# Key and value caches in layouts made by kernel(), outputs stored from the loaded tiles, tail reordered: one step of a two-layer decoder on one core

## The chip, the cores and the metric

The kernel runs on one core of one Trainium2 chip. The core has TensorE (PE: matmuls, with a weight load PEld for each), VectorE (DVE), ScalarE (ACT), GpSimd (POOL) and SyncE (SP). SP issues nearly all DMAs here, in its program order; the DMAs then run on the core's 16 DMA engines. The metric is device time in microseconds, from start to end of one execution. What kernel() does with numpy on the host, before and after the launch, isn't in it.

## The reference

One inference step for a prompt of 256 tokens (with 16 learned meta tokens ahead of it, 272 positions) and for a group of 8 samples of one token each. Layer 0 is an RWKV-7 mixer, layer 1 is sliding-window attention with grouped queries and sinks. Both layers have width 4096 (model width 2048), and each branch is gated. All data is fp32.

```python
if i == N_A_LAYERS - 1:
    kp, vp = shared_kv(hp, kv_norm, w_kv, pos_p)          # prompt: keys after rotary, values
    ksn, vsn = shared_kv(hs, kv_norm, w_kv, pos_s)        # samples: the new key and value
    k_all = jnp.concatenate([cache_k.astype(ksn.dtype), ksn], axis=1)   # (8, 128 + 1, 8, 64)
    v_all = jnp.concatenate([cache_v.astype(vsn.dtype), vsn], axis=1)
...
q, z = jnp.split(rmsnorm(hp, b_norm[j]) @ b_w_qz[j], 2, axis=-1)
q = rotary(q.reshape(B, L, N_Q_HEADS, HEAD_DIM), pos_p)
att = banded_prompt_attention(q, kp, vp, sinks)
hp = hp + (att * jax.nn.silu(z)) @ b_w_o[j]
...
att = sink_attend(q, k_all, v_all, valid_s, sinks).reshape(DB, S_dec, WIDTH)
hs = hs + (att * jax.nn.silu(z)) @ b_w_o[j]
...
y_prompt = rmsnorm(hp, final_norm)[:, N_META:]
y_sample = rmsnorm(hs, final_norm)
p_cache_k = kp[:, -win:]
p_cache_v = vp[:, -win:]
s_cache_k = k_all[:, -win:]
s_cache_v = v_all[:, -win:]
```

The cache that goes in has 128 positions for each sample, 8 key heads of 64 and as many values. The cache that goes out has the same size: the oldest position is dropped, the new one is put at the end. Queries are 64 heads, 8 to each key head.

## The kernel before

**Products.** Every large product is made with split fp32: a weight tile of 256 x 256 (256 KB, `raw`) is loaded by SP (L192 in `wunits`), ACT rounds it to `whi` (L177), VectorE makes the rest `wlo` (L178), and `mm3` does three matmuls, high by high, high by low, low by high (L199, L200, L201). A tile, called a unit here, is worth 12 matmuls. There are 4 buffers of raw (8 in most of the attention part, with the second pool `rawx`) and 5 each of whi and wlo, so ACT and VectorE work a few units ahead of TensorE, and SP about eight ahead.

**Stages.** `phase_a` is the RWKV mixer, `out_a` its output product. `phase_b` makes the shared keys and values: four products of `kv`, then for each pair of key heads `rotate` on VectorE (`stream_shuffle`, three operations; the result is the tile `rout_k`), and copies to `KT` (keys transposed, 64 rows twice, 280 positions). Keys come out of the product with head dimension on the partitions. For the outputs that want position on the partitions, TensorE transposes them (`ps_kt`, L1446 and L1447, against the identity in `consts`), VectorE copies the result to `ktk` and `ksn` (L1448, L1449), and SP stores those.

**Attention.** `phase_b2` runs the query and gate products (q, z) and, in between, a generator `heads`: for each of 8 groups (key heads) and each half of a group, two planes of scores (`ps_s`), a softmax on VectorE and ACT, the transposes of the probabilities (`ps_pt`) and the values (`ps_at`). TensorE's order here is the order in which the generators are run, written out by hand; `yield 5`, say, is five steps of the product, half a unit each. `end_q` rotates a plane of queries on VectorE as soon as its product is done; the scores of the plane wait for that.

The samples' attention is `attend_cache(g)`, run in five parts by `heads`. The first part loads the cache of group g (`kc` and `vc`, 128 positions on the partitions, L1718 and L1719) and copies 127 positions of sample g from the input cache to the output cache, DRAM to DRAM (L1723). The second spreads the queries (`qz`), transposes kc (`ps_kc`, L1737, four matmuls), copies the result to `kTc` by ACT (L1739) and puts the new key into kTc's last column by VectorE (L1742). The third makes scores (`ps_dc`, L1746) and their softmax (`dm`, `dSB`). The fourth transposes the probabilities (`ps_dp`), the fifth makes the values (`ps_da`). There are two buffers of kc and vc, one of kTc.

**What sets the order elsewhere.** On VectorE, ACT, GpSimd and SP, and on TensorE outside the handwritten stretches, a scheduler with a cost model orders the instructions at build time. Each engine then runs its list strictly in order: what stands behind a waiting instruction waits too.

**The tail.** `out_b` is the last output product, 16 column blocks k, two to a product. For each it adds the residual, squares (`sqb`, ACT), sums the squares of blocks 0 to 14 on GpSimd (`sqacc`, L1804), transposes the block (`ps_h`, L1807) and scales it into `ht` (L1810). Row sums of squares come from matmuls with ones (`ps_stb`, L1813): one set for sqacc at k = 14, one for the last block's squares at k = 15. Then an inverse root by VectorE, a scaling of ht[0] by VectorE (L1823) and of ht[1] by ACT (L1825) in two halves of 1024 columns, and the stores (L1824, L1826, L1828).

Of the kernel before, what the change touches and what calls it, by code (L numbers as in the profile page):

```python
# [10 lines left out]
F32 = mybir.dt.float32  # L11
# [13 lines left out]
NS = 8  # L25
# [78 lines left out]
class Kernel:  # L104
# [1300 lines left out]
    def phase_b(self):  # L1405
# [21 lines left out]
        with self.tc.tile_pool(name="kvm", bufs=2, reuse_waits="tile") as pool:  # L1427
# [3 lines left out]
            dma(cs, I['consts'][:, C_COS:C_COS + 2 * N].rearrange("p (a n) -> p a n", a=2))  # L1431
            ksn, ktk = (pool.tile([r, 512], F32, tag=n, bufs=1, name=n) for r, n in ((NS, "ksn"), (128, "ktk")))
            tt(cosr, cs[:, 0], self.rb, op=MU)
            tt(sinr, cs[:, 1], self.rb, op=MU)
            for c in range(4):
                if c % 2 == 0:
                    pss = self.gemm(I['w_kv'][0], "kv", KT, c * 128, x)
                    self.pump(c == 2)
                ps = pss[c % 2]
                kr = self.rotate(pool, ps, cosr, sinr, N, f"k{c}")  # L1440
                for h in range(2):
                    s = slice(64 * h, 64 * h + 64)
                    for q in range(2):
                        (V.tensor_copy if q else A.copy)(self.KTd[2 * c + h][64 * q:64 * q + 64], kr[s])
                pt = self.bank(self.pe, f"ps_kt{c}")
                nc.tensor.transpose(pt[:, 0:128], kr[:, 144:272], self.ident)  # L1446
                nc.tensor.transpose(pt[:NS, 128:256], kr[:, L:N], self.ident)  # L1447
                V.tensor_copy(ktk[:, c * 128:c * 128 + 128], pt[:, 0:128])  # L1448
                V.tensor_copy(ksn[:, c * 128:c * 128 + 128], pt[:NS, 128:256])  # L1449
            for c in range(4):  # L1450
# [18 lines left out]
            dma(self.Vm[16:32, :, 64:128], self.Vm[:16, :, 0:64])  # L1469
            f = lambda n: O[n].rearrange("b w h d -> b w (h d)")  # L1470
            dma(f('p_cache_k')[0], ktk)
            dma(f('p_cache_v')[0], self.Vd)
            dma(f('s_cache_k')[:, WIN - 1], ksn)
            dma(O['s_cache_v'][:, WIN - 1], self.Vn[0:64:8, :, 0])
            self.bmx = [self.norm_mix(bp, "bm", P_BN, k) for k in range(KT)]
# [236 lines left out]
    def attend_cache(self, g):  # L1712

        nc, bp, I = self.nc, self.bp, self.I
        V, A = nc.vector, nc.scalar
        kc = bp.tile([128, NS, 64], F32, tag="kc", bufs=2, name=f"kc{g}")
        vc = bp.tile([128, NS, 64], F32, tag="vc", bufs=2, name=f"vc{g}")
        nc.sync.dma_start(kc, I['cache_k'][:, :, g].rearrange("b w d -> w b d"))  # L1718
        nc.sync.dma_start(vc, I['cache_v'][:, :, g].rearrange("b w d -> w b d"))  # L1719
        for n in 'kv':  # L1720
            row = lambda a: a[g].rearrange("w h d -> w (h d)")
            self.tc.keep_in_program_order(
                nc.sync.dma_start(row(self.O['s_cache_' + n])[0:WIN - 1], row(I['cache_' + n])[1:WIN]))  # L1723
        yield
# [4 lines left out]
        for o in range(2):  # L1729
            for h in range(2):  # L1730
                c = 8 * o + h
                V.tensor_copy(qz.rearrange("p (s c) -> p s c", c=144)[64 * o:64 * o + 64, :, c:c + 8:2],
                              qs[64 * h:64 * h + 64, o])
        kT = bp.tile([128, NS // 2, 129], F32, tag="kTc", name=f"kTc{g}")
        pk = self.bank(self.py, f"ps_kc{g}")
        for i in range(4):
            nc.tensor.transpose(pk[:, 128 * i:128 * i + 128], kc[:, 2 * i:2 * i + 2].rearrange("p b d -> p (b d)"),  # L1737
                                self.ident)
        A.copy(kT[:, :, 0:128], pk.rearrange("p (b w) -> p b w", b=4))  # L1739
        for o in range(2):  # L1740
            r = slice(64 * o, 64 * o + 64)
            V.tensor_copy(kT[r, :, 128], self.KTd[g][r, L + o:N:2])  # L1742
        yield
        pd = self.bank(self.py, f"ps_dc{g}")[:, :129]
# [34 lines left out]
    def out_b(self):  # L1779
# [11 lines left out]
        for k in range(KT):  # L1791
# [8 lines left out]
            if k == 0:  # L1800
                acc = pool.tile([128, NB], F32, name="sqacc")
                nc.gpsimd.tensor_copy(acc, sq)
            elif k < KT - 1:
                nc.gpsimd.tensor_tensor(acc, acc, sq, op=ALU.add)  # L1804
# [3 lines left out]
            for i, r in enumerate(rows):  # L1808
                s = slice(128 * k, 128 * k + 128)
                V.tensor_tensor(ht[i][:r, s], pt[:r, 128 * i:128 * i + 128], fn[:r, s], op=ALU.mult)  # L1810
            if k >= KT - 2:
                for i, r in enumerate(rows):
                    nc.tensor.matmul(pst[i][:r, 0:2], (acc if k == KT - 2 else sq)[:, 128 * i:128 * i + r], one,  # L1813
                                     start=k == KT - 2, stop=k == KT - 1)
        rs = pool.tile([128, 3], F32, name="rsf")
# [4 lines left out]
        outs = (O['y_prompt'][0, 0:128], O['y_prompt'][0, 128:256], O['y_sample'].rearrange("b o d -> (b o) d"))  # L1820
        for c in range(2):
            s = slice(D // 2 * c, D // 2 * c + D // 2)
            V.tensor_scalar(ht[0][:, s], ht[0][:, s], rs[:, 0:1], None, op0=ALU.mult)  # L1823
# [8 lines left out]
    ('y_prompt', (1, SEQ, D)), ('y_sample', (NS, 1, D)), ('p_state_wkv', (1, 1, 64, 64, 64)),  # L1832
    ('p_state_shift', (1, 1, D)), ('p_cache_k', (1, WIN, NKV, HD)), ('p_cache_v', (1, WIN, NKV, HD)),
    ('s_state_wkv', (1, NS, 64, 64, 64)), ('s_state_shift', (1, NS, D)),
    ('s_cache_k', (NS, WIN, NKV, HD)), ('s_cache_v', (NS, WIN, NKV, HD)),
]
# [7 lines left out]


# [16 lines left out]
```

## Time and profile before

| | |
|---|---|
| median of 3 runs | 2201.3 us (2196.46, 2201.3, 2201.85) |
| the profiled execution's own time | 2204.44 us |
| its span, first to last instruction | 2202.5 us |
| mean granted TensorE clock | 0.987 |
| DMA moved | 455.40 MB, 207 GB/s over the span |

| stage, us of the span | what |
|---|---|
| 0 to 1456 | start, RWKV mixer and its output product |
| 1456.8 to 1515.1 | keys and values |
| 1515.1 to 1997.3 | q and z products, with attention from 1529 to 1901 |
| 1997.3 to 2188.3 | last output product |
| 2188.3 to 2202.5 | tail |

How to read it: the page gives busy time by engine, in sum and by stretch; PEclk is the clock that TensorE was granted, as a share of full speed. Matmuls are pipelined, so one may stand for 0.28 us while the next starts 0.12 us after it. Rows of the timeline are: start, how long, engine, line, operation, tiles out and in, shapes, count, and in brackets the idle time ahead of it with what ended that. Rows of waits are: who waited for what, microseconds in total, times, longest. In lists of instructions, "x32: 271/272/273" is the count and the shortest, median and longest nanoseconds. Rows that start with a stretch (A:B) give busy time of PE, PEld, DVE, ACT and POOL in it, then clock, DMA's share and GB/s.

### The profile page before, as it was taken

The numbers are of one execution on the slowest core, as the hardware profiler recorded it, in microseconds if no ns is written. First come the engines' busy times: TensorE is split into PE (matmuls) and PEld (weight loads), VectorE is DVE, ScalarE is ACT, GpSimd is POOL, SyncE is SP. The second block draws the span as 40 slices with busy tenths as digits, with TensorE's granted clock in tenths as the row PEclk, the third lists the DMA queues.
The fourth block names the chain that finished last, engine by engine and source line by source line (L and its number), as shares of the span: only waits on it lengthen the run. The fifth ranks groups of instructions, "written<-read, shape, count | busy, mean of one in ns | idle before, by whom it ended". The sixth has DMA issues, their size and how long they took to land. (4 is left out here: it accounts for less than half of the span.)

```text
span 2202.5 us, 56367 instructions
## 1 busy us (share of the span) xinstructions
PE 2124.8 (96%) x21596; PEld 2015.7 (92%) x21596; DVE 1710.4 (78%) x4138; ACT 1284.0 (58%) x2961; POOL 76.5 (3%) x102
## 2 busy tenths in 40 slices
PE   6999999999999999989999999999999999999997
PEld 4899889899999899989988999999999999999997
DVE  5875757687678677689877787887888888888885
ACT  3546766577676666667766544565555556555443
POOL 0010000000000000000100000110000000000000
PEclk9999999999999999999999999999999999999999
DMA  7978566668676658766655868777554544577774
GB/s 239 340 260 257 173 229 210 198 174 266 204 220 187 188 187 268 239 208 184 200 175 150 283 177 278 240 212 207 163 159 140 163 150 134 163 212 242 229 226 136
DMA packets 289718, 455.40 MB, mean 207 GB/s; under 512 B 64280, under 2 KB 112984, under 8 KB 289056
## 3 DMA queue, kind: packets, MB, share of 16 engines
q1 hardware_dynamic: 288632, 449.51, 66.0%
q8 instruction: 169, 2.77, 0.5%
q10 hardware_dynamic: 816, 2.29, 0.3%
q14 instruction: 101, 0.83, 0.1%
HBM read 385.08 MB, written 70.73 MB: 207 GB/s over the span
## 5 line engine op out<-in xcount | busy, mean ns | idle before, releaser
L199 PE MATMUL ps_z<-mhlm,whi_z 128*128 128x280 f32 x512 | 160.0, 312 | 0.0
L201 PE MATMUL ps_z<-mhlm,wlo_z 128*128 128x280 f32 x512 | 151.5, 296 | 0.8 <-DVE wlo_z L178 0.8
L199 PE MATMUL ps_q<-bmh,whi_qb 128*128 128x264 f32 x512 | 150.0, 293 | 1.5 <-ACT whi_qb L177 1.5
L200 PE MATMUL ps_z<-mhlm,whi_z 128*128 128x280 f32 x512 | 151.2, 295 | 0.0
L199 PE MATMUL ps_z<-bmh,whi_zb 128*128 128x264 f32 x512 | 147.5, 288 | 0.0
L201 PE MATMUL ps_q<-bmh,wlo_qb 128*128 128x264 f32 x512 | 145.8, 285 | 1.1 <-DVE wlo_qb L178 1.1
L200 PE MATMUL ps_q<-bml,whi_qb 128*128 128x264 f32 x512 | 145.6, 284 | 0.0
L200 PE MATMUL ps_z<-bml,whi_zb 128*128 128x264 f32 x512 | 145.5, 284 | 0.0
L201 PE MATMUL ps_z<-bmh,wlo_zb 128*128 128x264 f32 x512 | 145.4, 284 | 0.0
L199 PE MATMUL ps_ob<-ghi,whi_ob 128*128 128x264 f32 x512 | 145.3, 285 | 0.0
L201 PE MATMUL ps_ob<-ghi,wlo_ob 128*128 128x264 f32 x512 | 144.8, 285 | 0.0
L200 PE MATMUL ps_ob<-glo,whi_ob 128*128 128x264 f32 x512 | 144.5, 283 | 0.0
L177 ACT CAST whi_ob<-raw_ob 128x512 fp32r<-128x512 f32 x128 | 79.2, 621 | 97.1 <-PE ps_ob L200 82.1
L178 DVE TENSOR_TENSOR wlo_r<-raw_r,whi_r 128x512 fp32r<-128x512 f32 x128 | 86.8, 686 | 57.1 <-ACT whi_r L177 51.7
L177 ACT CAST whi_oa<-raw_oa 128x512 fp32r<-128x512 f32 x128 | 78.3, 620 | 87.2 <-DMA raw_oa<-a_w_out 27.1
L178 DVE TENSOR_TENSOR wlo_v<-raw_v,whi_v 128x512 fp32r<-128x512 f32 x128 | 86.7, 685 | 50.8 <-ACT whi_v L177 49.2
L199 PE MATMUL ps_v<-mhlm,whi_v 128*128 128x280 f32 x384 | 121.9, 317 | 0.0
L199 PE MATMUL ps_k<-mhlm,whi_k 128*128 128x280 f32 x384 | 121.2, 316 | 0.0
L178 DVE TENSOR_TENSOR wlo_k<-raw_k,whi_k 128x512 fp32r<-128x512 f32 x112 | 76.5, 690 | 56.8 <-ACT whi_k L177 54.8
L177 ACT CAST whi_zb<-raw_zb 128x512 fp32r<-128x512 f32 x128 | 78.3, 620 | 62.5 <-PE ps_z L200 41.1
L178 DVE TENSOR_TENSOR wlo_z<-raw_z,whi_z 128x512 fp32r<-128x512 f32 x128 | 86.5, 683 | 36.3 <-ACT whi_z L177 36.0
L200 PE MATMUL ps_k<-mhlm,whi_k 128*128 128x280 f32 x384 | 113.8, 296 | 0.0
(479 smaller groups left out, 7726.0 us busy)
## 6 DMA issues: line engine op xcount, KB each, us to landing
raw_k<-a_w_rkvz SPq DMA_DIRECT2D x128, 256.0 KB
raw_v<-a_w_rkvz SPq DMA_DIRECT2D x128, 256.0 KB
raw_r<-a_w_rkvz SPq DMA_DIRECT2D x128, 256.0 KB
raw_z<-a_w_rkvz SPq DMA_DIRECT2D x128, 256.0 KB
raw_oa<-a_w_out SPq DMA_DIRECT2D x128, 256.0 KB
raw_qb<-b_w_qz SPq DMA_DIRECT2D x128, 256.0 KB
raw_zb<-b_w_qz SPq DMA_DIRECT2D x128, 256.0 KB
raw_ob<-b_w_o SPq DMA_DIRECT2D x128, 256.0 KB
```

The source lines that it names most:

```text
L177: self.nc.scalar.copy(hi, src)
L178: return self.nc.vector.tensor_tensor(lo, src, hi.bitcast(F32), op=ALU.subtract)
L199: mm(ps, wh, xh, start=start, stop=False)
L200: mm(ps, wh, xl, start=False, stop=False)
L201: return mm(ps, wl, xh, start=False, stop=stop)
```

## The change

On the host, kernel() now puts cache_k into the layout [group, 128, 4, 129]: head dimension of two samples on the 128 partitions, four pairs of samples, 128 positions and one column of padding. cache_v goes to [group, position, sample, 64]. The outputs p_cache_k, s_cache_k and s_cache_v have layouts of that kind too, and `returned` puts them back on the host.

In the kernel:

- `attend_cache` loads kTc itself, in one DMA (two buffers of kTc, none of kc). The four transposes and ACT's copy are gone. The copies of the new key into column 128 (VectorE) stay; they now follow a load into the same tile.
- The DRAM to DRAM copies are gone. s_cache_v's 127 old positions are stored from the loaded vc, s_cache_k is stored from kTc with the new key in it, columns 1 to 128.
- `phase_b` stores p_cache_k from `rout_k`, without transposes and without ktk and ksn, in four DMAs; the single store of the samples' new keys goes.
- In `out_b`, GpSimd sums the squares of blocks 0 to 13 (0 to 14 before) into sqacc. The matmuls with ones follow at k = 13 for sqacc, at k = 14 and at k = 15 for those blocks' own squares: three sets, where there were two. The scaling and the stores of ht[0] and ht[1] are split at column 512 instead of 1024.

```diff
-            ksn, ktk = (pool.tile([r, 512], F32, tag=n, bufs=1, name=n) for r, n in ((NS, "ksn"), (128, "ktk")))
...
-                pt = self.bank(self.pe, f"ps_kt{c}")
-                nc.tensor.transpose(pt[:, 0:128], kr[:, 144:272], self.ident)
-                nc.tensor.transpose(pt[:NS, 128:256], kr[:, L:N], self.ident)
-                V.tensor_copy(ktk[:, c * 128:c * 128 + 128], pt[:, 0:128])
-                V.tensor_copy(ksn[:, c * 128:c * 128 + 128], pt[:NS, 128:256])
+                dma(O['p_cache_k'][c], kr[:, 144:272])
...
-            f = lambda n: O[n].rearrange("b w h d -> b w (h d)")
-            dma(f('p_cache_k')[0], ktk)
-            dma(f('p_cache_v')[0], self.Vd)
-            dma(f('s_cache_k')[:, WIN - 1], ksn)
-            dma(O['s_cache_v'][:, WIN - 1], self.Vn[0:64:8, :, 0])
+            dma(O['p_cache_v'][0].rearrange("w h d -> w (h d)"), self.Vd)
+            dma(O['s_cache_v'][:, WIN - 1].rearrange("g b d -> b g d"), self.Vn[0:64:8, :, 0])
...
-        kc = bp.tile([128, NS, 64], F32, tag="kc", bufs=2, name=f"kc{g}")
+        kT = bp.tile([128, NS // 2, 129], F32, tag="kTc", bufs=2, name=f"kTc{g}")
         vc = bp.tile([128, NS, 64], F32, tag="vc", bufs=2, name=f"vc{g}")
-        nc.sync.dma_start(kc, I['cache_k'][:, :, g].rearrange("b w d -> w b d"))
-        nc.sync.dma_start(vc, I['cache_v'][:, :, g].rearrange("b w d -> w b d"))
-        for n in 'kv':
-            row = lambda a: a[g].rearrange("w h d -> w (h d)")
-            self.tc.keep_in_program_order(
-                nc.sync.dma_start(row(self.O['s_cache_' + n])[0:WIN - 1], row(I['cache_' + n])[1:WIN]))
+        nc.sync.dma_start(kT.rearrange("p s w -> p (s w)"), I['cache_k'][g])
+        nc.sync.dma_start(vc, I['cache_v'][g])
+        nc.sync.dma_start(self.O['s_cache_v'][g, 0:WIN - 1], vc[1:WIN])
         yield
...
-        kT = bp.tile([128, NS // 2, 129], F32, tag="kTc", name=f"kTc{g}")
-        pk = self.bank(self.py, f"ps_kc{g}")
-        for i in range(4):
-            nc.tensor.transpose(pk[:, 128 * i:128 * i + 128], kc[:, 2 * i:2 * i + 2].rearrange("p b d -> p (b d)"),
-                                self.ident)
-        A.copy(kT[:, :, 0:128], pk.rearrange("p (b w) -> p b w", b=4))
         for o in range(2):
             r = slice(64 * o, 64 * o + 64)
             V.tensor_copy(kT[r, :, 128], self.KTd[g][r, L + o:N:2])
+        nc.sync.dma_start(self.O['s_cache_k'][g], kT[:, :, 1:129])
         yield
...
-            elif k < KT - 1:
+            elif k < KT - 2:
                 nc.gpsimd.tensor_tensor(acc, acc, sq, op=ALU.add)
...
-            if k >= KT - 2:
+            if k >= KT - 3:
                 for i, r in enumerate(rows):
-                    nc.tensor.matmul(pst[i][:r, 0:2], (acc if k == KT - 2 else sq)[:, 128 * i:128 * i + r], one,
-                                     start=k == KT - 2, stop=k == KT - 1)
+                    nc.tensor.matmul(pst[i][:r, 0:2], (acc if k == KT - 3 else sq)[:, 128 * i:128 * i + r], one,
+                                     start=k == KT - 3, stop=k == KT - 1)
...
-        for c in range(2):
-            s = slice(D // 2 * c, D // 2 * c + D // 2)
+        for s in (slice(0, D // 4), slice(D // 4, D)):
             V.tensor_scalar(ht[0][:, s], ht[0][:, s], rs[:, 0:1], None, op0=ALU.mult)
             nc.sync.dma_start(outs[0][:, s], ht[0][:, s])
...
+def returned(r):
+
+    r = dict(r)
+    r['p_cache_k'] = r['p_cache_k'].reshape(NKV, HD, WIN).transpose(2, 0, 1)[None]
+    k = r['s_cache_k'].reshape(NKV, 2, HD, NS // 2, WIN).transpose(3, 1, 4, 0, 2)
+    r['s_cache_k'] = k.reshape(NS, WIN, NKV, HD)
+    r['s_cache_v'] = r['s_cache_v'].transpose(2, 1, 0, 3)
+    return tuple(r[k] for k, _ in OUTS)
...
+    k = arrays['cache_k'].reshape(NS // 2, 2, WIN, NKV, HD).transpose(3, 1, 4, 0, 2).reshape(NKV, 128, NS // 2, WIN)
+    arrays['cache_k'] = np.pad(k, ((0, 0), (0, 0), (0, 0), (0, 1))).reshape(NKV, 128, -1)
+    arrays['cache_v'] = np.ascontiguousarray(arrays['cache_v'].transpose(2, 1, 0, 3))
```

The order of instructions moves with it. On TensorE, in the attention part, the only difference is that the four transposes are gone; the place is that of group 2, between the two column blocks of a z product. Before:

```order
L200 MATMUL ps_z_2_24832<-bml_23181,whi_zb_10_24885 128x264
L201 MATMUL ps_z_2_24832<-bmh_23180,wlo_zb_10_24886 128x264
L1737 MATMUL ps_kc_25022<-consts,kc_24808 128x128 x4
L199 MATMUL ps_z_3_24833<-bmh_23168,whi_zb_8_24848 128x264
L200 MATMUL ps_z_3_24833<-bml_23169,whi_zb_8_24848 128x264
```

and now:

```order
L199 MATMUL ps_z_2_24797<-bmh_23160,whi_zb_10_24850 128x264
L200 MATMUL ps_z_2_24797<-bml_23161,whi_zb_10_24850 128x264
L201 MATMUL ps_z_2_24797<-bmh_23160,wlo_zb_10_24851 128x264
L199 MATMUL ps_z_3_24798<-bmh_23148,whi_zb_8_24813 128x264
L200 MATMUL ps_z_3_24798<-bml_23149,whi_zb_8_24813 128x264
```

The product goes straight on from one column block to the next.

VectorE at the start of the attention part, where the first two planes of queries (q, from ps_q_0 and ps_q_1) are rotated ahead of the first scores. Before:

```order
L178 TENSOR_TENSOR wlo_qb_2_23371<-raw_qb_2_23368,whi_qb_2_23370 128x512
L1628 STREAM_SHUFFLE rtmp_q_0_23393<-ps_q_0_23234 128x264
L1630 TENSOR_TENSOR q_23392<-ps_q_0_23234,cosr 128x264
L1629 TENSOR_TENSOR rtmp_q_0_23393<-rtmp_q_0_23393,sinr 128x264
L1631 TENSOR_TENSOR q_23392<-q_23392,rtmp_q_0_23393 128x264
L1628 STREAM_SHUFFLE rtmp_q_1_23410<-ps_q_1_23235 128x264
L1630 TENSOR_TENSOR q_23392<-ps_q_1_23235,cosr 128x264
L1629 TENSOR_TENSOR rtmp_q_1_23410<-rtmp_q_1_23410,sinr 128x264
L1631 TENSOR_TENSOR q_23392<-q_23392,rtmp_q_1_23410 128x264
L178 TENSOR_TENSOR wlo_qb_4_23383<-raw_qb_4_23380,whi_qb_4_23382 128x512
L178 TENSOR_TENSOR wlo_qb_6_23420<-raw_qb_6_23417,whi_qb_6_23419 128x512
```

and now (kTc_24103 is group 1's tile):

```order
L178 TENSOR_TENSOR wlo_qb_4_23362<-raw_qb_4_23359,whi_qb_4_23361 128x512
L1620 STREAM_SHUFFLE rtmp_q_0_23372<-ps_q_0_23214 128x264
L1622 TENSOR_TENSOR q_23371<-ps_q_0_23214,cosr 128x264
L1621 TENSOR_TENSOR rtmp_q_0_23372<-rtmp_q_0_23372,sinr 128x264
L178 TENSOR_TENSOR wlo_qb_6_23399<-raw_qb_6_23396,whi_qb_6_23398 128x512
L1620 STREAM_SHUFFLE rtmp_q_1_23389<-ps_q_1_23215 128x264
L1622 TENSOR_TENSOR q_23371<-ps_q_1_23215,cosr 128x264
L1623 TENSOR_TENSOR q_23371<-q_23371,rtmp_q_0_23372 128x264
L178 TENSOR_TENSOR wlo_qb_8_23411<-raw_qb_8_23408,whi_qb_8_23410 128x512
L1621 TENSOR_TENSOR rtmp_q_1_23389<-rtmp_q_1_23389,sinr 128x264
L1725 COPY kTc_24103<-KT_22359 64x4 x2
L1623 TENSOR_TENSOR q_23371<-q_23371,rtmp_q_1_23389 128x264
```

Two weight splits (wlo_qb_6 and wlo_qb_8) and the copy of group 1's new key stand among the rotations, ahead of the last add.

VectorE and SP where the samples' scores of group 1 are reduced (dm) and the cache tile of a later group is prepared. VectorE before:

```order
L1750 TENSOR_REDUCE dm_24460<-ps_dc_24454 128x1
L1742 COPY kTc_25021<-KT_22360 64x4 x2
L1751 TENSOR_TENSOR dm_24460<-dm_24460,snd 128x1
L1752 TENSOR_TENSOR dm_24460<-snd,dm_24460 128x1
L1753 TENSOR_SCALAR dm_24460<-dm_24460 128x1
```

VectorE now, and SP now:

```order
L1734 TENSOR_REDUCE dm_24426<-ps_dc_24420 128x1
L1735 TENSOR_TENSOR dm_24426<-dm_24426,snd 128x1
L1736 TENSOR_TENSOR dm_24426<-snd,dm_24426 128x1
L1737 TENSOR_SCALAR dm_24426<-dm_24426 128x1
L1725 COPY kTc_25449<-KT_22361 64x4
L1740 TENSOR_TENSOR dm_24426<-dm_24426 128x1
L1725 COPY kTc_25449<-KT_22361 64x4
```

```order
L192 DMA raw_zb_12_24661<-b_w_qz 128x512
L1710 DMA kTc_25449<-cache_k 128x516
L192 DMA raw_zb_14_24685<-b_w_qz 128x512
L192 DMA raw_zb_0_24697<-b_w_qz 128x512
L1726 DMA s_cache_k<-kTc_25449 512x1x128
L192 DMA raw_zb_2_24734<-b_w_qz 128x512
```

Before, the copy belonged to group 2's tile and stood behind nothing but the reduce of group 1; now it belongs to group 3's tile, whose load stands on SP six weight tiles later than kc's load did, with the store that needs the copy two weight tiles behind it.

More of the change, by code (lines that the diff above doesn't have):

```diff
@@ L1832 @@
     ('y_prompt', (1, SEQ, D)), ('y_sample', (NS, 1, D)), ('p_state_wkv', (1, 1, 64, 64, 64)),
-    ('p_state_shift', (1, 1, D)), ('p_cache_k', (1, WIN, NKV, HD)), ('p_cache_v', (1, WIN, NKV, HD)),
+    ('p_state_shift', (1, 1, D)), ('p_cache_k', (4, 128, WIN)), ('p_cache_v', (1, WIN, NKV, HD)),
     ('s_state_wkv', (1, NS, 64, 64, 64)), ('s_state_shift', (1, NS, D)),
-    ('s_cache_k', (NS, WIN, NKV, HD)), ('s_cache_v', (NS, WIN, NKV, HD)),
+    ('s_cache_k', (NKV, 128, NS // 2, WIN)), ('s_cache_v', (NKV, WIN, NS, HD)),
 ]
@@ L1860 @@
     r = run_bass_kernel_spmd(nc, [arrays], core_ids=[0])
-    return tuple(r.results[0][k] for k, _ in OUTS)
+    return returned(r.results[0])
```

## The prediction, made before the changed kernel was run

> **What bounds the kernel now.** I read the page's first part, then busy time by stage, then TensorE's waits.
>
> ```profile
> PE 2124.8 (96%) x21596; PEld 2015.7 (92%) x21596; DVE 1710.4 (78%) x4138; ACT 1284.0 (58%) x2961; POOL 76.5 (3%) x102
> 1610.90:1910.00 299.10, 299.10 (x2563) 288.19 (x2562) 247.75 (x915) 176.30 (x476) 0.00 (x0) 1.00 0.49 147
> 1997.30:2188.30 191.00, 191.00 (x1581) 190.69 (x1581) 150.78 (x272) 85.34 (x144) 12.67 (x15) 1.00 0.68 211
> ```
>
> TensorE is busy 96% of the span, and all of the two stretches below it: most of the attention part and the last product. DMA is at about half and two thirds there. So an instruction taken from TensorE is worth its own time unless the engine then waits for its operands; work taken from ACT, VectorE or DMA is worth nothing by itself. TensorE's waits from 1450 us on, in all:
>
> ```profile
> PE ps_kv L199 <- ACT whi_kv L177: 1.6, 2, 1.4
> PE ps_q L199 <- ACT whi_qb L177: 1.5, 1, 1.5
> PE ps_q L201 <- DVE wlo_qb L178: 1.1, 3, 0.5
> PE ps_kv L201 <- DVE wlo_kv L178: 0.6, 1, 0.6
> ```
>
> Where it waits, it waits for split weights (whi by ACT, wlo by VectorE), and only 4.8 us in all. The rest is throughput.
>
> **The change part by part: the 32 transposes of cached keys.** The tile's group, then TensorE's sequence around one of the eight sets:
>
> ```profile
> L1737 PE MATMUL ps_kc<-consts,kc x32: 271/272/273, 1545.8 to 1862.3; 128*128 128x128 f32 x32
> ...
> 1861.94 0.60 PE L1737 MATMUL ps_kc<-consts,kc 128*128 128x128 f32 x4
> 1862.29 0.37 PE L199 MATMUL ps_z<-bmh,whi_zb 128*128 128x264 f32 x1
> 1862.50 0.28 PE L200 MATMUL ps_z<-bml,whi_zb 128*128 128x264 f32 x1
> ```
>
> Matmuls overlap, so starts count, not durations. The set begins at 1861.94, the product goes on at 1862.29, and its second matmul starts at 1862.50, where 0.12 would do. So a set holds TensorE 0.56 - 0.12 = 0.44 us, and eight hold it 3.5 us. (By durations it would be 32 x 272 ns = 8.7 us: a rival below. The Trainium skill, "TensorE: Matmul & The Clock Gate", Part 4: PE-mode transpose, gives about 275 ns for a transpose in a kernel; the duration here agrees, the starts do not let it count. By the Trainium skill's figure alone these would be 8.8 us.)
>
> Not all of the 3.5 us stays. After each softmax the next split weight is barely ready:
>
> ```profile
> 1638.45 0.69 DVE L178 TENSOR_TENSOR wlo_zb<-raw_zb,whi_zb 128x512 fp32r<-128x512 f32 x1
> 1639.47 0.28 PE L201 MATMUL ps_z<-bmh,wlo_zb 128*128 128x264 f32 x1
> 1864.13 0.68 DVE L178 TENSOR_TENSOR wlo_zb<-raw_zb,whi_zb 128x512 fp32r<-128x512 f32 x1
> 1864.87 0.39 PE L201 MATMUL ps_z<-bmh,wlo_zb 128*128 128x264 f32 x1
> ```
>
> Group 2's weight is ready at 1639.14 and used at 1639.47: 0.33 us to spare. Group 7's is ready at 1864.81 and used at 1864.87, by a matmul that stands 0.39 instead of 0.28: it waited already. The sets lie just ahead of these points, so TensorE arrives 0.44 us earlier and meets VectorE, whose softmax chain starts from the scores and isn't shortened. Kept per set: from 0 to 0.44, 0 to 3.5 us in all; I take 0.19, between the two pairs shown, so 1.5 us. ACT's eight copies of the result and the py bank's use cost nothing before and give nothing.
>
> **The prompt keys' eight transposes.**
>
> ```profile
> 1486.76 0.27 PE L1446 MATMUL ps_kt<-consts,rout_k 128*128 128x128 f32 x1
> ...
> 1486.89 0.38 PE L199 MATMUL ps_kv<-kvh,whi_kv 128*128 128x280 f32 x1
> 1487.11 0.29 PE L200 MATMUL ps_kv<-kvl,whi_kv 128*128 128x280 f32 x1
> ```
>
> From 1486.76 to 1487.11 is 0.35 us with one product matmul of 0.13 inside: 0.22 us a pair, four pairs 0.9 us. Bounds 0 (the product then waits for weights) and 0.9; I take 0.9, the stage after 1479 us having no wait in the list. VectorE's eight copies go too. The four new stores of rout_k sit on SP between weight loads and wait for VectorE's rotation, which in the order stands about where SP arrives; the next raw tiles are eight deep, so 0. The rout buffer, two deep, is rewritten one product later, long after a store.
>
> **The first group of attention.** Here the order changes most.
>
> ```profile
> 1529.11 0.43 DVE L1631 TENSOR_TENSOR q<-q,rtmp_q 128x264 f32<-128x264 f32 x1
> ...
> 1529.26 1.62 PE L1645 MATMUL ps_s<-KT,q 64*128 64x256 f32 x16
> 1539.89 0.39 PE L199 MATMUL ps_q<-bmh,whi_qb 128*128 128x264 f32 x1 [1.51 <-ACT whi_qb L177]
> 1540.85 0.39 PE L201 MATMUL ps_q<-bmh,wlo_qb 128*128 128x264 f32 x1 [0.45 <-DVE wlo_qb L178]
> 1542.31 0.39 PE L201 MATMUL ps_q<-bmh,wlo_qb 128*128 128x264 f32 x1 [0.46 <-DVE wlo_qb L178]
> ...
> 1523.39 0.96 SPq L1723 DMA_DIRECT2D s_cache_k<-cache_k  x1
> 1525.08 1.94 SPq L192 DMA_DIRECT2D raw_qb<-b_w_qz  x4
> ...
> 1529.59 2.06 ACT L177 CAST whi_qb<-raw_qb 128x512 fp32r<-128x512 f32 x3 [4.82 <-DVE q L1631]
> ```
>
> TensorE loses 1.51 + 0.45 + 0.46 = 2.4 us of waiting, and the first matmul after each wait stands 0.39 instead of 0.28 us: 2.7 us. The weights are late because the raw tiles issued at 1525.08 lie behind the cache copies (DRAM to DRAM, issued from 1523.39) and ACT casts the first only at 1529.59, and because the casts after that stand behind the softmax's exponentials. Now those copies are gone, two more casts stand ahead of the exponentials, and raw tiles are issued ahead of the stores. Against it, VectorE has two weight splits (0.69 each) and a key copy (0.34) ahead of the second plane's last rotation add, which ends at 1529.54 now. That is 1.72 us later, and TensorE stands at the scores from 1529.26: it waits up to about 1.2 us more, the first plane's scores being done meanwhile. I take 2.7 - 1.2 = 1.5 us gained; bounds 2.7 gained, and 2 lost (the old waits stay, and 2 us are waited at the scores).
>
> **The new loads, copies and stores of groups 2 to 7.** VectorE's copy of the new key into kTc now needs the tile's load landed, and s_cache_k's store on SP needs that copy, with weight loads queued behind it. Load of group g needs ps_dc of g - 2 done.
>
> ```profile
> 1646.49 0.28 DVE L1750 TENSOR_REDUCE dm<-ps_dc 128x1 f32<-128x129 f32 x1
> ...
> 1647.44 0.15 DVE L1753 TENSOR_SCALAR dm<-dm 128x1 f32<-128x1 f32 x1
> ...
> 1650.46 0.69 DVE L178 TENSOR_TENSOR wlo_qb<-raw_qb,whi_qb 128x512 fp32r<-128x512 f32 x1 [0.76 <-ACT whi_qb L177]
> 1652.65 1.42 DVE L178 TENSOR_TENSOR wlo_qb<-raw_qb,whi_qb 128x512 fp32r<-128x512 f32 x2 [1.51 <-PE ps_q L200]
> ...
> 1637.24 0.38 SPq L1718 DMA_DIRECT2D kc<-cache_k  x1
> ...
> 1639.50:1640.00 0.50, 0.50 (x7) 0.50 (x6) 0.50 (x4) 0.50 (x2) 0.00 (x0) 1.00 0.29 65
> ...
> SPq L1718 <- PE ps_kc L1737: 33.2, 6, 6.8
> ```
>
> The old kc load, issued at 1637.24, moved its last bytes near 1639.7: 2.5 us. SP can issue the new load when the reduce can start, at 1646.5 or a little earlier, so it lands near 1648.8; where the copy follows the reduce's third small operation (ends 1647.59) VectorE waits 1.2 us, part of it a wait for ACT that was there. It then has 0.76 and 1.51 us idle, 2.3 together, before the next scores. So 0 for TensorE, bounds 0 and the 1.2 us in all six groups, 7.2 us lost. SP, held up to 33.2 us by the old kc loads without a wait at TensorE after 1610, is held by loads and stores instead: 0. The 16 DRAM copies go; DMA isn't the bound: 0.
>
> **The tail.**
>
> ```profile
> 2188.91 0.73 PE L1813 MATMUL ps_stb<-one,sqacc 128*128 128x2 f32 x6 [0.15 <-POOL sqacc L1804]
> 2189.58 0.55 PE L1807 MATMUL ps_h<-consts,h 128*128 128x128 f32 x3
> 2189.96 0.63 PE L1813 MATMUL ps_stb<-one,sqb 128*128 128x2 f32 x6
> ...
> 2193.03 1.42 DVE L1823 TENSOR_SCALAR ht<-ht,rsf 128x1024 f32<-128x1024 f32 x2
> ```
>
> A third set of sums costs 2189.58 - 2188.91 = 0.67 us inside the last product. The second no longer waits for GpSimd: it can follow the transposes, 0.3 us earlier. The first store can leave after 512 columns instead of 1024, a quarter instead of half of 1.42 us: 0.36 us earlier, and the stores run back to back after it. 0.67 - 0.3 - 0.36 = 0; bounds 0.7 each way.
>
> **Sum.** 1.5 + 0.9 + 1.5 + 0 + 0 = 3.9 us off. The profiled execution took 2204.4 us, so 2200.5 against its own time; it stands 3.1 us above the median of 2201.3, so 2197.4 for the median. That is 0.18%; about 0.3% (6.6 us) is what a measurement of this kernel can tell from no change.
>
> **Rivals.** (1) The gains are whole: 3.5 + 0.9 + 2.7 + 0.7 = 7.8 us, 2193.5. For it: VectorE's order moves splits ahead of softmax work in three groups. Against it: the pairs above. (2) Durations are the price: 40 transposes by 272 ns are 10.9 us, 2190.4. Against it: the starts. (3) Nothing is left: VectorE's chain sets the pace of the attention part, the wait at the scores eats the first group's gain, and the clock may drop:
>
> ```profile
> 1468.00:1471.80 3.80, 2.19 (x15) 1.75 (x14) 2.04 (x4) 3.79 (x10) 0.00 (x0) 1.00 0.56 126
> 1471.80:1478.60 6.80, 6.16 (x26) 5.70 (x25) 6.38 (x17) 3.34 (x7) 0.52 (x1) 0.50 0.59 175
> 1536.00:1543.00 7.00, 4.57 (x33) 3.94 (x32) 5.19 (x20) 5.40 (x20) 0.00 (x0) 1.00 0.38 120
> ```
>
> After 1.6 us of idle within 3.8 the granted clock was 0.50 for 6.8 us, which costs 3.4; after 2.4 us within 7.0 it stayed 1.00. A wait at the scores could bring that on: 3.9 less 3.4, and 2200 to 2203. (The Trainium skill, the same page, section Part 1: The HAM clock gate, lets the clock fall after an idle window of about 3.4 us; no wait here is so long, and the row at 1468 fell with less, so I keep the 3.4 us as possible. By the page's rule this part would be 0.) (4) Slower: kTc's load lands late and VectorE, in order, holds every weight split behind the copy. It reaches the copy about 1.4 us after ps_dc's end and has those 2.3 us to spare; each of six groups loses landing time - 3.7. At 2.5 us that is nothing; at 5.5 it is 10.8 us and, with the 3.9 gained, 6.9 slower, about the point from which it decides; at 6.0 us it is 13.8, 9.9 slower, 2211. For it: the raw tiles of 1525.08 took 4.5 us. Against it: those lay behind the DRAM copies, which go.
>
> **Chances.** Forecast 0.46, (1) 0.24, (2) 0.03, (3) 0.18, (4) 0.09. Faster by over 0.3%: (1) and (2), 0.27. Within: 0.64. Slower: 0.09. Range 2190.5 to 2203.0: (2) below, (3) above; (4) is left out.
>
> **What would show it.** Each step: starts of 0.12 us across the old sets; waits for wlo after softmax, 0.1 to 0.4 us each, where the gain is lost; one wait at ps_s near 1530 and none at 1539; VectorE waiting for cache_k near each dm reduce, up to 1.2 us; POOL gone from the waits at ps_stb. The prediction is wrong if the wait for cache_k reaches TensorE, if the scores of the first group wait over 3 us, or if the clock falls in new places.

## The result, and the profile after

The changed kernel takes 2214.1 us (median of 4 runs, 2210.9 to 2216.5), the kernel before 2201.6 (4 runs, 2196.5 to 2203.9). The ratio is 1.0061, 95% interval 1.0046 to 1.0076: slower by 0.6%, some 13 us, where 0.18% faster was forecast.

The first part of the changed kernel's page, busy time by engine:

```profile
PE 2124.8 (96%) x21562; PEld 2013.3 (91%) x21562; DVE 1708.5 (77%) x4130; ACT 1279.4 (58%) x2953; POOL 75.4 (3%) x101
```

The busy time is nearly that of before, in a span that is 12 us longer (2214.4 for 2202.5). So something waits. TensorE's waits from 1450 us on, then VectorE's waits at the copy of the new key (who waited for what, us in all, times, longest):

```profile
PE ps_s L1637 <- DVE q L1623: 13.2, 2, 10.0
PE ps_dp L1747 <- DVE at L1702: 1.8, 2, 1.2
...
DVE kTc L1725 <- DMA kTc<-cache_k: 23.3, 7, 9.3
```

Two waits at the first scores make 13.2 us, one of them 10.0. What stands there on VectorE and on SP's queue, and then on TensorE, in the timeline of the changed kernel:

```profile
1528.85 0.43 DVE L1621 TENSOR_TENSOR rtmp_q<-rtmp_q,sinr 128x264 f32<-128x264 f32 x1
1538.53 0.34 DVE L1725 COPY kTc<-KT 64x4 f32<-64x4 f32 x2 [9.25 <-DMA kTc<-cache_k]
1538.91 0.43 DVE L1623 TENSOR_TENSOR q<-q,rtmp_q 128x264 f32<-128x264 f32 x1
...
1523.65 0.43 SPq L1712 DMA_DIRECT2D s_cache_v<-vc  x1
1524.18 4.61 SPq L192 DMA_DIRECT2D raw_qb<-b_w_qz  x1
1528.84 0.56 SPq L1710 DMA_DIRECT2D kTc<-cache_k  x1
...
1528.48 0.95 PE L1637 MATMUL ps_s<-KT,q 64*128 64x256 f32 x8 [3.25 <-DVE q L1623]
1539.40 1.70 PE L1637 MATMUL ps_s<-KT,q 64*128 64x256 f32 x8 [9.97 <-DVE q L1623]
```

VectorE stands at group 1's copy for 9.25 us; behind it is the last add of the second plane's rotation, and TensorE waits for that add. The load that the copy waits for was issued at 1528.84 and landed 9.7 us later. The prediction's rows gave 2.5 us for such a load.

The trace also records when each part of a DMA has landed. Fifteen of this load's sixteen parts were in by 1531.76, the last at 1538.51. The weight tile issued right behind the store of s_cache_v is the same: fifteen parts by 1531.05, the last at 1537.86. The store itself, issued at 1523.65, has, behind one early record, a single one, at 1537.22. So one sixteenth of what is issued behind the store comes after it.

Busy time in three stretches (PE, PEld, DVE, ACT, POOL, then clock, DMA's share, GB/s) shows what the DMA engines did meanwhile:

```profile
1526.50:1529.00 2.50, 0.52 (x5) 0.55 (x7) 2.50 (x8) 0.18 (x1) 0.00 (x0) 1.00 0.07 25
1530.00:1535.00 5.00, 0.00 (x0) 0.00 (x0) 0.00 (x0) 0.00 (x0) 0.00 (x0) 0.50 0.88 299
1535.00:1538.50 3.50, 0.00 (x0) 0.00 (x0) 0.00 (x0) 0.00 (x0) 0.00 (x0) 0.50 0.07 28
```

A share of 0.07 is about one engine of sixteen, and 25 to 28 GB/s is what it moves. While everything waits, from 1535.0 to 1538.5, one DMA engine works and fifteen have nothing to do; in the trace's list of packets, most of those in it are of 2 KB and take 84 ns, one after another. The clock is at 0.50. Such stretches (one or two engines busy, 1.5 us or longer, from 1455 to 2190 us) add up to some 59 us; in the kernel before to less than 5.

The trace, cut into stages by TensorE's first and last matmul of each kind, in us. "First group" runs from the first q product to the samples' first scores (ps_dc), "groups" from there to their last; the runs below stand in the same table.

| kernel | kv | first group | groups | to last product | last product | tail | sum |
|---|---|---|---|---|---|---|---|
| before | 58.24 | 39.16 | 317.05 | 125.99 | 190.76 | 14.33 | 745.5 |
| changed | 57.08 | 53.12 | 318.69 | 126.01 | 191.47 | 14.06 | 760.4 |
| e1, 128 rows | 56.90 | 40.56 | 317.91 | 126.01 | 191.47 | 14.10 | 747.0 |
| e2, copy on GpSimd | 57.01 | 54.87 | 315.74 | 126.01 | 191.47 | 14.25 | 759.4 |
| e3, both | 57.05 | 42.27 | 315.81 | 126.01 | 191.47 | 14.07 | 746.7 |
| e4, before with the 127-row store | 57.97 | 52.12 | 317.05 | 125.99 | 190.76 | 14.33 | 758.2 |
| e5, 112 and 15 rows | 57.11 | 42.74 | 318.71 | 126.01 | 191.47 | 14.10 | 750.1 |
| e6, before with keys and tail | 57.00 | 41.66 | 317.19 | 125.99 | 191.44 | 14.05 | 747.3 |
| e7, e3 with transposes | 56.90 | 41.81 | 316.81 | 126.01 | 191.47 | 14.09 | 747.1 |
| e8, e3 with value stores on GpSimd | 56.81 | 38.37 | 315.72 | 126.01 | 191.47 | 14.26 | 742.6 |
| e9, e8 with two sets of sums | 56.91 | 37.61 | 315.83 | 126.01 | 190.80 | 14.50 | 741.7 |
| e10, e9 with all cache DMAs on GpSimd | 56.89 | 38.55 | 315.78 | 126.01 | 190.80 | 14.60 | 742.6 |

The sums leave out what lies ahead of the kv stage. The instructions there stand in the same order in all of these kernels, but for two neighbours on VectorE in some, and it took 1445 to 1457 us in these executions: most of the scatter of the whole times arises there, and so differences of 1 to 4 us are read from the stages. Each row is one execution (e3's was the slowest of its ten, e9's the fastest of its twelve). The groups of e3 and of e8 to e10 agree within some 0.1 us; the first groups of e8 and e9, in which the engines' instructions stand in the same order, differ by 0.8, so less than that isn't read from a first group. The 14.9 us of the changed kernel are 14.0 in the first group, 1.6 in the groups and 0.4 at the end, less 1.2 in kv.

### The profile page after: what moved, and what is told of

The parts are those of the page before. It is cut to its first block, busy times and chain, and to the rows that moved or that the text cites. A ratio compares the mean times of both kernels' runs of the same rounds, so it can differ in the third digit from the quotient of the medians.

```text
span 2214.4 us, 56292 instructions
## 1 busy us (share of the span) xinstructions
PE 2124.8 (96%) x21562; PEld 2013.3 (91%) x21562; DVE 1708.5 (77%) x4130; ACT 1279.4 (58%) x2953; POOL 75.4 (3%) x101
## 4 chain that ended last, share of the span: by engine, by line
PE 79%; DMA 8%; DVE 7%; ACT 3%; issue 2%; SPq 0%; POOL 0%; DVEq 0%; ACTq 0%; POOLq 0%
PE ps_z L199 5%; PE ps_z L201 5%; PE ps_z L200 5%; PE ps_k L199 3%; PE ps_ob L201 3%; PE ps_ob L200 3%; PE ps_ob L199 3%; PE ps_v L199 3%; PE ps_k L201 3%; PE ps_k L200 2%; PE ps_v L200 2%; PE ps_v L201 2%; PE ps_q L199 2%; PE ps_q L201 2%; PE ps_q L200 2%; PE ps_r L199 2%
```

## The experiments

**Theory A**: the store of s_cache_v's old positions, 127 rows of vc, runs on one DMA engine, and what is queued behind it there lands late. **Theory B**: the load is late because of its place among the others, whatever the row count.

**e1: 128 rows.** The output has one more position, which the host drops.

```diff
-        nc.sync.dma_start(self.O['s_cache_v'][g, 0:WIN - 1], vc[1:WIN])
+        nc.sync.dma_start(self.O['s_cache_v'][g, 0:WIN], vc)
```

> The changed kernel, with s_cache_v stored from all 128 rows of vc (the output holds one more position, dropped on the host) instead of 127. Theory A: the 127-row store runs on a single DMA engine (127 packets of 84 ns are 10.7 us), and group 1's kTc load lies behind it; then that load lands some 2.8 us after its issue, as group 0's did, VectorE's wait at the copy falls from 9.3 to about 2.5 us, TensorE's at the scores from 10.0 to about 3, the half clock after 1529.9 goes, and the time is about 2205. Stretches in which only one or two DMA engines work, 59 us after 1455 now, fall below 10. Theory B: the load is late because of where it stands among the other loads; the row count changes nothing, 2214.

Measured 2199.4 us, ratio to before 1.0002 (0.9989 to 1.0014). Stretches with one or two engines: less than 5 us. The same place in e1, the wait at the first scores, and the copy's waits:

```profile
1520.00:1522.00 2.00, 2.00 (x19) 2.00 (x18) 0.26 (x1) 0.43 (x1) 0.00 (x0) 1.00 1.01 347
1522.00:1526.00 4.00, 1.38 (x12) 1.20 (x12) 3.78 (x11) 1.43 (x3) 0.00 (x0) 1.00 0.97 294
...
PE ps_s L1637 <- DVE q L1623: 3.2, 2, 2.6
DVE kTc L1725 <- DMA kTc<-cache_k: 12.4, 7, 2.9
```

All DMA engines work, the longest wait at the copy is 2.9 us instead of 9.3, TensorE's two at the scores 3.2 together. One row more takes some 13 us off (1.0061 to 1.0002): theory A. TensorE, VectorE, ACT and SP run the first group in the same order as in the changed kernel, so the row count alone makes the difference there: 12.6 us. It went further than the 2205 expected. TensorE's second wait fell from 9.97 to 0.63 us, not to 3, the first from 3.25 to 2.62, and the half clock lasted 3.4 us instead of 13.7.

**e2: the copy on GpSimd, 127 rows kept.**

```diff
-            V.tensor_copy(kT[r, :, 128], self.KTd[g][r, L + o:N:2])
+            nc.gpsimd.tensor_copy(kT[r, :, 128], self.KTd[g][r, L + o:N:2])
```

> The changed kernel, with the copy of the new key into kTc done by GpSimd instead of VectorE; the 127-row store stays. If VectorE, held in order at the copy, is what carries a late load to TensorE, the waits of 3.5 and 10.0 us at the first scores and the half clock go although the load lands as late as now: 2198 to 2203, a rest being weights that SP issues late behind the store of kTc. If the late load hurts by another way (weights of the same DMA engine), TensorE waits for weights instead and the time stays above 2208.

Measured 2212.1 us, 1.0066 (1.0051 to 1.0081). VectorE waits at no copy now, and it is as slow as the changed kernel. TensorE's waits in e2:

```profile
PE ps_q L199 <- ACT whi_qb L177: 8.9, 3, 6.1
PE ps_s L1637 <- DVE q L1623: 3.5, 2, 3.2
```

The second outcome written down came true. The store hurts by another way when the first is shut: ACT waits for weight tiles (20.2 us for raw_qb in the attention part, 4.1 in the kernel before), since one sixteenth of each lies behind the store: of the tile issued at 1523.65, fifteen parts were in by 1527.44, the last at 1533.57. VectorE's wait was one way in which the loss came out, not its cause.

**e3: both edits.**

The two diffs above together:

```diff
+        nc.sync.dma_start(self.O['s_cache_v'][g, 0:WIN], vc)
...
+            nc.gpsimd.tensor_copy(kT[r, :, 128], self.KTd[g][r, L + o:N:2])
```

> The changed kernel with both edits: 128 rows, and the copy on GpSimd. Theory A: all that was lost in the first group (3.5 + 10.3 us, some 2 us of half clock) and the 1.8 us at the transposed probabilities come back, about 2197, what the sum of the prediction gave. If the kept part of the transposes was really nothing, 2200 to 2202.

Measured 2194.3 us, 0.9988 (0.9973 to 1.0003). That is near what was expected, but the interval reaches to no change, and its stages say 746.7 us against 745.5 before: the first group still takes 3.1 us longer.

**e4: the kernel before, with the 127-row store.** The value cache has the new layout; keys and tail are as before. The scheduler then also orders VectorE and ACT in the first group anew: three weight splits stand among the two rotations.

```diff
-        nc.sync.dma_start(vc, I['cache_v'][:, :, g].rearrange("b w d -> w b d"))
-        for n in 'kv':
+        nc.sync.dma_start(vc, I['cache_v'][g])
+        nc.sync.dma_start(self.O['s_cache_v'][g, 0:WIN - 1], vc[1:WIN])
+        for n in 'k':
```

> The kernel before with one part of the change alone: the value cache in the new layout, its 127 old positions stored from vc (127 rows) instead of copied in DRAM. Theory A: stretches with a single DMA engine show up for every group, about 50 us in all where there were 5, and weight tiles whose share lies behind the store land late: 1 to 6 us slower than before if the eight tiles of lead don't cover 10.7 us, else no change; no wait at a copy of kTc, since that follows the transposes. Theory B: no such stretches, no change.

Measured 2209.5 us, 1.0060 (1.0037 to 1.0084): this part, with the order that it brings, costs what the whole change lost, more than the 1 to 6 us expected. Its SP queue, a stretch of busy time, and ACT:

```profile
1515.69 1.33 SPq L192 DMA_DIRECT2D raw_qb<-b_w_qz  x3
...
1525.94 0.60 SPq L1720 DMA_DIRECT2D s_cache_v<-vc  x1
1526.63 10.25 SPq L192 DMA_DIRECT2D raw_qb<-b_w_qz  x1
1536.93 0.61 SPq L1724 DMA_DIRECT2D s_cache_k<-cache_k  x1
...
1529.20:1537.50 8.30, 7.84 (x54) 7.42 (x54) 3.11 (x15) 2.65 (x8) 0.00 (x0) 0.87 0.07 27
...
1546.02 0.62 ACT L177 CAST whi_qb<-raw_qb 128x512 fp32r<-128x512 f32 x1 [7.33 <-DMA raw_qb<-b_w_qz]
```

The issue of one weight tile behind the store takes SP 10.25 us, where three such issues took 1.33 just before. 127 rows of 2 KB at 25 GB/s are 10.4 us, so SP itself is held for about as long as the one engine needs for a store. What that alone costs isn't shown: the tile that ACT waits 7.33 us for is this one, and fifteen of its parts were in by 1538.98, the last at 1545.92, just behind the store of 1525.94 (1545.30). That is e2's way again. TensorE waits 5.5 us for casts and 3.1 at the scores, and the clock is at 0.50 twice for 6.8 us. In the groups after the first there are such stretches too, up to 5 us each, and they cost nothing (317.05 us, as before): there the tiles loaded ahead cover them.

**e5: 112 and 15 rows.**

```diff
-        nc.sync.dma_start(self.O['s_cache_v'][g, 0:WIN - 1], vc[1:WIN])
+        nc.sync.dma_start(self.O['s_cache_v'][g, 0:112], vc[1:113])
+        nc.sync.dma_start(self.O['s_cache_v'][g, 112:WIN - 1], vc[113:WIN])
```

> The changed kernel, with the 127 old positions of s_cache_v stored by two DMAs, of 112 and of 15 rows of vc; the output's layout and VectorE's copy stay. Theory A (the number of rows decides: a count that 16 divides spreads over 16 engines, 15 over 15, and 127 has no divisor up to 16 but 1): no stretches with a single DMA engine, as with 128 rows, and about 2199. Rival: any store that isn't a whole tile of 128 partitions lies on one engine; then 112 packets of 84 ns are 9.4 us and the time stays near 2213.

Measured 2201.2 us, 1.0017 (1.0000 to 1.0034); stretches with one or two engines less than 10 us. The same 127 rows, from the same partitions, cost nothing like that when two DMAs carry them. In the records of landings the store of 112 rows ends in 16 parts and, behind one early record, that of 15 rows in 15, all within 4.9 us of their issue. It is the count of rows in one DMA that decides, not that the tile isn't stored whole. The Trainium skill, "DMA: Bandwidth & Descriptors", section "Why a DMA increments its semaphore by 16 and not by 1", states that rule: a DMA uses the largest number of engines up to 16 that divides the size of the slowest dimension of both its sides, and it names 127 partitions as a case with one engine. The runs here agree: a share of 0.07 with 127 rows, 0.97 and 1.01 in e1's rows. The kernel before copied the same 127 positions from DRAM to DRAM, where they are contiguous and stand in the trace as 16 runs of 16256 bytes.

**e6: the kernel before with the keys' store and the tail alone.** The samples' new keys ride in the store of rout_k; attend_cache is untouched.

```diff
-                nc.tensor.transpose(pt[:, 0:128], kr[:, 144:272], self.ident)
-                nc.tensor.transpose(pt[:NS, 128:256], kr[:, L:N], self.ident)
...
+                dma(O['p_cache_k'][c], kr[:, 144:N])
```

> The kernel before with two parts of the change alone, the prompt keys' store from rout_k without transposes (the samples' new keys ride in the same store) and the tail's order; attend_cache is as before. Theory: the keys-and-values stage is 0.9 us shorter (57.8 to 56.9), the first group from the first q product to the samples' first scores stays at 39.2 us as before, since VectorE's two rotations stand together again, the last product is 0.7 longer and the tail 0.3 shorter: 0.5 off in all, no measurable change. Rival: the first group's loss of 1.4 to 3.1 us that the repaired kernels show comes from the earlier stage or from SP's stores of rout_k; then it is here too.

Measured 2199.4 us, 1.0000 (0.9984 to 1.0015). Keys and values 57.00 us, last product and tail as expected; but the first group takes 41.7 us and not 39.2, so the rival has a part in it: in this execution, whose engines run the first group in the order of before, the first group gives back what the shorter kv stage gains, and more. TensorE there waits once for a cast, and then runs at half clock:

```profile
PE ps_q L199 <- ACT whi_qb L177: 2.2, 1, 2.2
...
1538.50:1545.30 6.80, 6.42 (x27) 6.04 (x28) 6.39 (x19) 3.42 (x7) 0.00 (x0) 0.50 0.55 161
```

In these 6.8 us the product's matmuls start 0.22 us apart instead of 0.12, which costs some 3 us.

**e7: e3 with four transposes in each group**, of vc into a bank that nobody reads.

```diff
+        pk = self.bank(self.py, f"ps_kc{g}")
+        for i in range(4):
+            nc.tensor.transpose(pk[:, 128 * i:128 * i + 128], vc[:, 2 * i:2 * i + 2].rearrange("p b d -> p (b d)"),
+                                self.ident)
```

> The kernel with both edits (128 rows, the copy on GpSimd) and, in every group, four transposes of vc into a bank that nobody reads, where the transposes of kc stood. Theory: from the samples' first scores to their last, seven sets, it takes 1.2 us more, 317.0 instead of 315.8: TensorE's share that the softmax chain does not swallow, 0.18 a set. By starts it would be 7 x 0.44 = 3.1 us. If the 1.2 us came from the DRAM copies or from ACT's and VectorE's copies that went, it stays at 315.8.

Measured 2199.3 us, 0.9998 (0.9982 to 1.0013). The groups take 316.8 us, e3's 315.8, before's 317.05. Seven sets cost 1.0 us when put back and gave 1.24 when taken away: 0.14 to 0.18 a set, not the 0.44 that they hold TensorE.

**e8: e3 with the stores of p_cache_v and of the samples' new values issued by GpSimd.** In e3, VectorE has the split of a late weight tile ahead of the first rotation:

```profile
1524.88 0.69 DVE L178 TENSOR_TENSOR wlo_qb<-raw_qb,whi_qb 128x512 fp32r<-128x512 f32 x1 [4.37 <-ACT whi_qb L177]
1525.50 0.45 DVE L1620 STREAM_SHUFFLE rtmp_q<-ps_q 128x264 f32<-128x264 f32 x1
```

```diff
-            dma(O['p_cache_v'][0].rearrange("w h d -> w (h d)"), self.Vd)
+            nc.gpsimd.dma_start(O['p_cache_v'][0].rearrange("w h d -> w (h d)"), self.Vd)
...
+            nc.gpsimd.dma_start(O['s_cache_v'][:, WIN].rearrange("g b d -> b g d"), self.Vn[0:64:8, :, 0])
```

> The kernel with both edits, and the stores of p_cache_v and of the samples' new values issued by GpSimd instead of SP, so that SP reaches the weight tile qb_4 of the third product earlier. In the kernel with both edits VectorE has that tile's split ahead of the first rotation, the tile is issued 4 us after its eight predecessors and lands 5.4 us later, and TensorE waits 4.0 us at the first scores. Theory: the tile comes 1 to 3 us earlier, the wait falls to 1 to 3 us, and the first group comes back to 39 to 41 us: about 2192. Rival: the tile's landing is set by the DMA engines' load and not by SP; then the wait stays at 4.

Measured 2197.2 us, 0.9991 (0.9977 to 1.0005). The wait at the first scores is 2.6 us in two parts, no longer 4.0 in one; the clock stays at 1.00, and the first group takes 38.4 us, 3.9 less than e3's:

```profile
PE ps_s L1637 <- DVE q L1623: 2.6, 2, 1.5
...
1523.00:1528.50 5.50, 2.94 (x26) 2.44 (x25) 5.47 (x20) 1.24 (x2) 0.61 (x2) 1.00 1.05 363
```

Not all of that is the queue's doing. SP issues the tile 0.6 us earlier in the group (8.07 us after its start, 8.66 in e3), and it lands 1.9 us earlier, 4.0 us after its issue instead of 5.3. And the scheduler put the first plane's last add ahead of the next split, and ACT's casts behind the exponentials; what each of these gives isn't shown. By stages e8 is 2.9 us faster than before, 0.13%, a size that the whole times, with an interval of 0.14% each way, cannot show.

**e9: e8 with the tail's sums as before**, GpSimd adding up to block 14, the stores still split at 512.

```diff
-            elif k < KT - 2:
+            elif k < KT - 1:
                 nc.gpsimd.tensor_tensor(acc, acc, sq, op=ALU.add)
...
-            if k >= KT - 3:
+            if k >= KT - 2:
```

> The kernel with 128 rows, the copy on GpSimd and the value stores of the keys-and-values stage issued by GpSimd, and with the sums of the tail as before (GpSimd adds the squares of blocks 0 to 14, two sets of matmuls); the split of the stores at column 512 stays. Theory: the last product goes back from 191.5 to 190.8 us; of the tail's 0.3 us the split keeps some 0.3 if that was what moved it, none if it was the sums. About 0.7 less than with three sets, 742.0 us from the start of keys and values to the end where before had 745.5: 0.1 to 0.2% faster than before, 2195 to 2197.

Measured 2197.2 us, 0.9991 (0.9979 to 1.0003). The last product is back at 190.8, and the tail is 14.50, 0.24 longer than e8's. So of the changed tail, the sums take 0.24 us off it and 0.67 on; the split at 512 alone takes nothing off (14.50 against 14.33 before).

**e10: e9 with all of the cache's loads and stores issued by GpSimd.**

```diff
-        nc.sync.dma_start(kT.rearrange("p s w -> p (s w)"), I['cache_k'][g])
+        nc.gpsimd.dma_start(kT.rearrange("p s w -> p (s w)"), I['cache_k'][g])
```

(and so for vc and for both stores)

> The same, with all loads and stores of the samples' cache issued by GpSimd too, so that SP's queue holds weight tiles alone in the attention part. If SP's waits behind the cache's DMAs are what delays weights in the first group, its 38.4 us fall to 37 and the time by 1 us more; if the DMA engines' supply is the limit there (250 to 290 GB/s from 1510 to 1530 us), nothing changes; if descriptors that GpSimd writes get in VectorE's way or land later, the group from samples' scores to samples' scores grows over 45.1 us.

Measured 2197.3 us, 0.9998 (0.9987 to 1.0010). The first group takes 38.55 us, no less than e8's 38.37 and e9's 37.61; the groups stay at 315.8. So SP's queue is no longer what holds the first group. The DMA engines are busy there (a share of 0.90 from 1510 to 1523 us), which fits the second of the three outcomes written down. No kernel here is clearly faster than the one before; e9's stages add up to 3.9 us less.

## Why the prediction was wrong

**The step that failed** is in the part on the new loads, copies and stores: "SP ... is held by loads and stores instead: 0. The 16 DRAM copies go; DMA isn't the bound: 0." DMA's mean share was read, and the shape of the new store wasn't. The store that replaced the copy runs on one engine for about 10 us, eight times; e1 shows that, with the order of instructions the same, it costs 12.6 us in the first group, and that without it the loss is gone. That DMA was at about half on the mean says nothing of one engine. The loss fell on the first group, forecast at 1.5 us gained with 2 lost as the bound: it took 14.0 us more. All three signs of being wrong that the prediction names came: the wait for cache_k reached TensorE, the scores waited 13.2 us, and the clock fell in a new place.

**Rival (4)**, the late load of kTc with VectorE in order behind it, had the mechanism that the profile shows and a time (2211) near the measured one. That the times agree is luck: its place was groups 2 to 7, its condition was not why the load came late, and "those lay behind the DRAM copies, which go" was the wrong argument: what took their place was worse. e2 shows that even this mechanism was only the visible way.

**The first group**: 1.5 us gained was forecast, with "it waits up to about 1.2 us more" at the scores. With 128 rows, or two stores, e1, e3 and e5 still lose 1.4 to 3.6 us there, and the wait is 3.2 to 4.0. The two splits among the rotations were counted by their 0.69 us each. The one that moved ahead of both rotations, wlo of the tile qb_4, wasn't counted, and it waits 4.37 us for its tile (e3), which SP issues behind the value stores and group 0's loads. With these stores on another queue, and another order on VectorE, the group took 0.8 us less than before (e8), which is no more than two like executions differ by (e8 and e9). The half clock, put at 3.4 us in rival (3), came in e1, e3, e5, e6 and e7 too, and not in e8 to e10.

**The transposes of cached keys**: 0.19 of 0.44 us a set were forecast, 0.14 to 0.18 measured (e3, e7). Right, with its reason: TensorE then meets split weights that aren't ready. From the samples' first scores to their last, the steps from one product matmul to the next where the next needs wlo (616 in each kernel) add up to 76.65 us in e3 and 75.41 before: 1.24 us, 0.18 a set, comes back there. Rival (2), by durations, is out.

**The prompt keys**: 0.9 us forecast, 0.9 to 1.4 measured (57.97 and 58.24 to between 56.81 and 57.11). Right for its stage. That the next stage can give it back (e6) wasn't seen.

**Groups 2 to 7**: 0 forecast, with bounds 0 and 7.2; it is 2.1 us in e1 and 2.9 in the changed kernel, by comparison with e3 and e2. The term was mis-sized because of the landing time, taken as 2.5 us from kc's load. The timeline of the changed kernel has 3.65 us in group 5, on SP and on VectorE:

```profile
1701.93 0.33 SPq L1710 DMA_DIRECT2D kTc<-cache_k  x1
...
1705.58 0.16 DVE L1725 COPY kTc<-KT 64x4 f32<-64x4 f32 x1 [1.80 <-DMA kTc<-cache_k]
```

and 3.65 to 4.2 in the others. "each of six groups loses landing time - 3.7" was the right form: by it 0 to 0.5 us a group, 1.7 in all, of the 2.9 measured. TensorE meets it at the transposes of the samples' probabilities (ps_dp, 1.8 us of waits in the changed kernel, 1.1 in e1), which wait for a later instruction of VectorE.

**The tail**: 0 forecast, 0.44 lost (0.71 lost in the last product, 0.27 gained behind it). The third set costs what was said, the sums give 0.24 where 0.3 was said, and the split gives nothing where 0.36 was said. The first store is issued 4.99 us after the start of the last product's last matmul, 5.68 before, as forecast; the last bytes don't leave earlier by that, since the store of the samples' rows still follows VectorE's scaling of them:

```profile
2205.36 1.27 SPq L1807 DMA_DIRECT2D y_prompt<-ht  x2
2207.47 0.30 SPq L1811 DMA_DIRECT2D y_sample<-ht  x1
```

In the kernel before that last issue is 7.5 us after that matmul (2195.66), now 7.1.

## What to carry to other kernels

Read a DMA's shape as the queue has it, rows first: a store of 127 rows was one engine for 10 us; one of 128, or two of 112 and 15, landed in sixteen or fifteen parts within 5 us. A mean DMA share can't show that; stretches with a share of 0.07 while others wait can. And a stage that is made shorter only helps if what the next stage waits for comes sooner too: here the weight tiles.

## What the runs showed of the hardware

Behind the 127-row store, fifteen sixteenths of a load or of a weight tile landed some 7 us ahead of the last sixteenth (1531.76 and 1538.51 in the changed kernel). An issue on SP can be held there too: one weight tile's issue took 10.25 us in e4 and 4.61 in the changed kernel, where three took 1.33; what holds it isn't shown.

The clock in the first group fell to 0.50 in every profiled execution in which TensorE was idle for 2.2 us or more at one place (2.2 in e6, 2.6 in e1, 2.7 to 6.1 and 10.0 in the others), for 3.4 to 13.7 us; after idle times of 1.7 us at most it stayed at 1.00 (before, e8, e9, e10), and in e2 after one of 2.0 us too. The Trainium skill, "TensorE: Matmul & The Clock Gate", section "Part 1: The HAM clock gate", speaks of an idle window of about 3.4 us; here one of 2.2 us came ahead of it (e6), which is shorter; the runs do not show whether the idle time alone decides. At 0.50 the matmuls started 0.22 us apart, at 1.00 0.12.
